# The third attention unit of each layer crosses by DMA transpose, with GpSimd laying its halves apart

## The chip, the cores and the metric

The kernel runs on one core of a Trainium2 chip. The metric is the device time of one execution in microseconds. The four compute engines that matter here are TensorE (PE, with its weight loads PEld), VectorE (DVE), ScalarE (ACT) and GpSimd (POOL); SyncE (SP) issues most of the DMAs. Each engine works through its own queue in order and waits for the others by semaphores.

## The reference

Two decoder layers over 512 tokens of width 1024, all float32. Each layer is a SwiGLU block, a token mixer and a second SwiGLU block, each behind an RMS norm. The mixer projects to queries, keys, values and three convolution parts; 8 query heads of width 64 in 2 groups attend in blocks of 128 tokens to their own block and the one before:

```python
z = h @ w_in[l]
scores = jnp.einsum("bnqkgd,bnskd->bnkgqs", qb, k_band) * scale
scores = jnp.where(mask_b, scores + bias, -jnp.inf)
m = jnp.maximum(jnp.max(scores, axis=-1, keepdims=True), sink_l)
p = jnp.where(mask_b, jnp.exp(scores - m), 0.0)
denom = jnp.sum(p, axis=-1, keepdims=True) + jnp.exp(sink_l - m)
out = jnp.einsum("bnkgqs,bnskd->bnqkgd", p / denom, v_band)
conv_out = short_conv(...)          # B * causal 3-tap convolution of (C * h)
x = x + jnp.concatenate([attn_out, conv_out], axis=-1) @ w_out[l]
```

## The kernel before

Every float32 matrix product is made of three products of a high part (hi, a rounded copy made by ScalarE) and a low part (lo, the rest, made by VectorE): hi·hi, lo·hi and hi·lo. Weights come in by DMA as raw, become wh on ScalarE (L228, CAST) and wl on VectorE (L228, TENSOR_TENSOR), two groups ahead of their use; raw has 8 buffers, which it shares with the attention's probabilities p.

In the mixer the projection runs in steps of one product of 24 matmuls (a group of 128 output columns, L318, L319, L321, into acc). Between the steps the attention's work is laid by tables of step numbers: one *unit* is a block n of 128 queries for one group g of 4 heads. There are 8 units, `todo`, numbered 0 to 3 for group 0 and 4 to 7 for group 1. In the names of tiles a unit is layer_n_g: unit 1 is 0_1_0, unit 2 is 0_2_0, unit 3 is 0_3_0, unit 4 is 0_0_1, unit 5 is 0_1_1. At each step `attend` does, in this order, send, values, turn and scores of the units that the tables name.

- scores: 16 matmuls (L1554, L1555; 8 for block 0) into sc; VectorE adds the bias and takes the maximum (L1558, an ISA row in the order), negates it (nm, L1569), adds the sink (es, L1571); ScalarE takes the exponentials with their sums (L1575); VectorE adds and inverts the sums and scales p (L1583).
- turn: the probabilities are transposed, so that keys lie on the partitions. Units 0, 2, 4, 6 and 7 are turned by TensorE, four transposes of 128x128 for each of their two key blocks (one for block 0; L1616, pt). Units 1, 3 and 5 are sent: ScalarE lays the two 16-bit halves of each word apart (L1590, 128x2048, into crossing), SP issues one DMA transpose back into p (L1592), and at the turn step ScalarE joins the halves of each key block (L1601, 128x1024). Either way ScalarE then makes the high part ph (L1621) and VectorE the low part pl (L1622) for each key block.
- values: two matmuls for each key block, with ph and with pl (L1633, L1634, o); ScalarE copies half of o (ol, L1636), VectorE adds it into m (L1639).

Unit 4's turn is inside the product of step 11 (INSIDE), between two of its k steps. The convolution of the same steps is on VectorE (product with acc, tap L1712), ScalarE (L1709, L1711) and GpSimd (L1715, an add, and L1716, a multiply). A scheduler then orders each engine's queue within what the dependences allow. `issue_after` keeps the joins behind the last weights' cast, and `go_on` keeps the next step's weight splitting behind the last instruction that `attend` gives back.

Of the kernel before, what the change touches and what calls it, by code (L numbers as in the profile page):

```python
# [54 lines left out]
STREAM_BACK_AT = {9: 0, 11: 1, 16: 2, 18: 3}  # L55
SCORES_AT = (5, 6, 7, 8, 9, 10, 12, 13)

SEND_AT = {7: 1, 9: 3, 11: 5}
TURN_AT = (6, 9, 8, 11, 10, 13, 14, 15)
VALUES_AT = (7, 10, 9, 12, 11, 14, 15, 16)  # L60
INSIDE = (11, 4, 5)
WARM = 3
XT_TAGS = ("sc", "aux", "aux", "mm", "sc", "sc", "aux", "aux")
# [12 lines left out]
def trunk_kernel(  # L76
# [23 lines left out]
    nc = tc.nc  # L100
# [11 lines left out]
    def g2(name, dt=F32, shape=(P, S)):  # L112
        return work.tile(list(shape), dt, tag="g2", bufs=14, name=name)

    def g8(name, dt=F32R, shape=(P, 2, 2, S)):
        return work.tile(list(shape), dt, tag="g8", bufs=4, name=name)
# [18 lines left out]
    def words(ap):  # L135

        return ap.bitcast(U16).rearrange("p (n two) -> p two n", two=2)
# [1356 lines left out]
    def mix(l, norm, after):  # L1494
        q = [None] * NH

        mixed = [g8(f"m_{l}_{j}", F32, (P, KC // 2, S)) for j in range(2)]
# [37 lines left out]
        class Unit:  # L1535
# [49 lines left out]
            def send(self):  # L1585


                self.room = crossing[:, todo.index(self) // 2 % 2, :]
                halves = self.room.bitcast(U16).rearrange("p (two n) -> p two n", two=2)
                nc.scalar.copy(halves, words(self.p.rearrange("p h k -> p (h k)")))  # L1590
                self.turned = self.p.rearrange("p h k -> p (h k)").bitcast(U16)
                nc.sync.dma_start_transpose(  # L1592
                    self.turned.rearrange("p (c q) -> p c q", q=P),
                    halves.rearrange("p two n -> p (two n)"),
                )
# [11 lines left out]
            def turn(self):  # L1607

                self.pt = []
                for kb in range(self.lo // P, 2):  # L1610
                    if todo.index(self) in SEND_AT.values():
                        tp = self.join(kb)
# [30 lines left out]
        todo = [Unit(n, g) for g in range(NKV) for n in range(NT)]  # L1643
        crossing = g8(f"crossing_{l}", F32, (P, 2, 4 * 2 * P))

        def attend(step):

            done = None
            if step in SEND_AT:
                todo[SEND_AT[step]].send()  # L1650
            for at, stage in ((VALUES_AT, "values"), (TURN_AT, "turn"), (SCORES_AT, "scores")):
                if stage == "turn" and step + 1 == INSIDE[0]:
                    done = todo[VALUES_AT.index(step)].added
                    continue
                if step in at:
                    done = getattr(todo[at.index(step)], stage)() or done
            return done

        for j in range(NH // 2):
            acc = group(norm.h) if j else qacc  # L1660
            if j == 3:
                vv = take_values()
            qf = scaled(acc, f"qf_{l}_{j}", by=1.0 / 8.0)
            both = form(f"q_{l}_{j}", shape=(P, 2, S))
            qe, qo = both[:, 0, :], both[:, 1, :]
            nc.scalar.copy(qe[:HD, :], qf[:HD, :])
            nc.scalar.copy(qo[HD:, :], qf[HD:, :])
            nc.vector.tensor_sub(qe[HD:, :], qf[:HD, :], f32(qe[:HD, :]))
            nc.vector.tensor_sub(qo[:HD, :], qf[HD:, :], f32(qo[HD:, :]))
            q[2 * j], q[2 * j + 1] = qe, qo  # L1670
            attend(2 + j)
# [4 lines left out]
        step = 6  # L1676
# [9 lines left out]
        def go_on():  # L1686

            nonlocal step
            last = attend(step)
            if step == TURN_AT[-1]:  # L1690
                state["turned"] = last.ins
            step += 1
            with tc.issue_after(last.ins) if last else nullcontext():
                need_split(state["group"] - 1 + SPLIT_AHEAD + (step >= TURN_AT[-1]))

        for pair in range(2):
            cs = []
            for j in range(2):
                c = g2(f"cc_{l}_{pair}_{j}")
# [4 lines left out]
            for j in range(2):  # L1704
                c = 2 * pair + j
# [79 lines left out]
```

## Time and profile before

| | |
|---|---|
| median of 3 runs | 1626.99 us (1626.08 to 1627.02) |
| the profiled execution | 1626.19 us, its span 1624.4 us |
| TensorE's granted clock | 0.999 |
| PE busy | 1615.4 us, 99% |
| DVE busy | 1376.7 us, 85% |
| ACT busy | 1178.1 us, 73% |
| POOL busy | 216.5 us, 13% |
| transposes of p on TensorE (L1616) | 64, median 272 ns each, started back to back |
| sends (L1590), joins (L1601) | 6 of 1897 ns, 12 of 1359 ns |

Times in the timeline are microseconds from the span's start. A line of the timeline has the start, the duration, the engine, the line of the kernel, the operation, its output and input and how often it repeats; in brackets stands idle time of its engine just before it and what ended that. Instructions of one engine overlap a little, so the spacing of their starts is what one of them costs its engine. The first layer's mixer steps discussed here lie at 368 to 440 us, the second's at 1171 to 1243 us.

### The profile page before, as it was taken

What the parts mean: (1) busy time and instruction counts of PE and PEld (TensorE: products, weight loads), DVE (VectorE), ACT (ScalarE), POOL (GpSimd) and SP (SyncE); (2) the same over time, 40 slices, a digit from 0 to 9 for tenths busy, and PEclk for the clock granted to TensorE, in tenths of its full rate; (3) what the DMA queues carried; (4) which work ended last, traced back from release to release, by engine and by line L of the source; (5) the groups of instructions that cost most, each with busy time, mean ns of one, the idle gap of its engine ahead of it and who ended that gap; (6) DMA issues with size and microseconds to landing.
All of it is one profiled execution on the core that took longest, in us unless ns stands there. A gap on an engine that the chain in (4) does not pass through costs nothing.

```text
span 1624.4 us, 21158 instructions
## 1 busy us (share of the span) xinstructions
PE 1615.4 (99%) x7571; PEld 1349.4 (83%) x7571; DVE 1376.7 (85%) x1788; ACT 1178.1 (73%) x1511; POOL 216.5 (13%) x191
## 2 busy tenths in 40 slices
PE   9999999999999999999999999999999999999998
PEld 7888888888898888888888888888888988888887
DVE  7978798988899977798998777989688998678997
ACT  6677777857766677778866777788586767878665
POOL 1211111001211111111011111110012111111121
PEclk9999999999999999999999999999999999999999
DMA  9999989822597698999767999998136978999892
GB/s 270 212 232 209 220 207 226 233 59 78 143 227 175 177 225 214 218 214 225 218 144 182 224 215 226 215 221 217 42 91 156 233 149 219 225 223 222 241 230 72
DMA packets 306031, 313.92 MB, mean 193 GB/s; under 512 B 125501, under 2 KB 188549, under 8 KB 305925
## 3 DMA queue, kind: packets, MB, share of 16 engines
q1 hardware_dynamic: 265412, 230.90, 50.1%
q0 software_dynamic: 40048, 81.27, 29.3%
q8 instruction: 59, 0.97, 0.2%
q14 instruction: 48, 0.39, 0.1%
q10 hardware_dynamic: 464, 0.40, 0.1%
HBM read 264.29 MB, written 2.10 MB: 164 GB/s over the span
## 4 chain that ended last, share of the span: by engine, by line
PE 98%; DVE 1%; DMA 0%; SPq 0%; issue 0%; ACT 0%; DVEq 0%
PE x L842 27%; PE y L842 13%; PE x_s L842 9%; PE acc L318 7%; PE acc L319 7%; PE acc L321 7%; PE w L842 7%; PE y_s L842 5%; PE x_m L827 3%; PE w_s L842 3%; PE y_m L827 1%; PE y_e L842 1%; PE acc L699 1%; PE x_e L842 1%; PE w_m L827 1%; PE sc L1555 0%
## 5 line engine op out<-in xcount | busy, mean ns | idle before, releaser
L228 DVE TENSOR_TENSOR wl<-raw,wh 128x1024 fp32r<-128x1024 f32 (+1 forms) x494 | 598.6, 1219 | 162.8 <-ACT wh L228 161.9
L228 ACT CAST wh<-raw 128x1024 fp32r<-128x1024 f32 (+1 forms) x494 | 514.1, 1044 | 304.6 <-PE x L842 92.8
L318 PE MATMUL acc<-xh,wh 128*128 128x512 f32 x392 | 153.3, 393 | 0.5 <-ACT wh L228 0.5
L319 PE MATMUL acc<-xl,wh 128*128 128x512 f32 x392 | 153.1, 391 | 0.0
L321 PE MATMUL acc<-xh,wl 128*128 128x512 f32 x384 | 149.7, 390 | 0.0
L223 POOL DMA_DIRECT2D raw<-in_ffn_wu_dram x40 | 50.6, 1272 | 381.6 <-DMA raw<-in_ffn_wu_dram 268.6
L318 PEld LDWEIGHTS acc<-xh,wh 128*128 128x128 f32 x392 | 73.8, 188 | 15.0 <-ACT wh L228 0.6
L319 PEld LDWEIGHTS acc<-xl,wh 128*128 128x128 f32 x392 | 73.7, 188 | 14.5
L321 PEld LDWEIGHTS acc<-xh,wl 128*128 128x128 f32 x384 | 72.1, 188 | 15.3
L223 POOL DMA_DIRECT2D raw<-in_ffn_wd_dram x34 | 41.0, 1218 | 272.0 <-DMA raw<-in_ffn_wd_dram 122.3
L223 POOL DMA_DIRECT2D raw<-in_ffn_wg_dram x40 | 49.1, 1237 | 201.9 <-DMA raw<-in_ffn_wu_dram 84.7
L269 DVE TENSOR_TENSOR raw<-raw,raw 128x1024 f32<-128x1024 f32 x58 | 70.5, 1220 | 1.7 <-DMA raw<-in_ffn_wu_dram 1.2
L1106 ACT COPY raw_a<-turned 128x1024 uint16<-128x1024 uint16 x48 | 63.5, 1357 | 0.0
L842 PE MATMUL x<-wl,ft1h 128*128 128x512 f32 x160 | 62.4, 390 | 0.0
L842 PE MATMUL w<-wh,fb21h 128*128 128x512 f32 x160 | 62.3, 390 | 0.0
L842 PE MATMUL y<-wh,ft3h 128*128 128x512 f32 x160 | 62.3, 390 | 0.0
L842 PE MATMUL x<-wh,ft1l 128*128 128x512 f32 x160 | 62.3, 389 | 0.0
L842 PE MATMUL x<-wl,ft2h 128*128 128x512 f32 x160 | 62.3, 389 | 0.0
L842 PE MATMUL x<-wh,ft2l 128*128 128x512 f32 x160 | 62.3, 389 | 0.0
L842 PE MATMUL x<-wh,ft1h 128*128 128x512 f32 x160 | 62.3, 389 | 0.0
L842 PE MATMUL w<-wh,fb21l 128*128 128x512 f32 x160 | 62.2, 389 | 0.0
L842 PE MATMUL y<-wh,ft3l 128*128 128x512 f32 x160 | 62.2, 389 | 0.0
(517 smaller groups left out, 4545.2 us busy)
## 6 DMA issues: line engine op xcount, KB each, us to landing
raw<-in_ffn_wu_dram SPq DMA_DIRECT2D x127, 512.0 KB, 5.6
raw<-in_ffn_wd_dram SPq DMA_DIRECT2D x105, 512.0 KB, 5.6
raw<-in_ffn_wg_dram SPq DMA_DIRECT2D x86, 512.0 KB, 5.3
raw<-in_ffn_wu_dram POOLq DMA_DIRECT2D x40, 512.0 KB, 9.1
raw<-in_ffn_wg_dram POOLq DMA_DIRECT2D x40, 512.0 KB, 6.5
raw<-in_w_in_dram SPq DMA_DIRECT2D x36, 512.0 KB, 4.0
raw<-in_ffn_wd_dram POOLq DMA_DIRECT2D x34, 512.0 KB, 8.2
raw<-in_w_out_dram SPq DMA_DIRECT2D x20, 512.0 KB, 4.6
```

Source lines behind the costliest of these rows:

```text
L223: nc.gpsimd.dma_start(out=r, in_=rows_of(*more), accum_op=ALU.add)
L228: return nc.scalar.copy(hi, raw), eng.tensor_sub(lo, raw, f32(hi))
L269: nc.vector.tensor_add(a11, a11, s1)
L318: nc.tensor.matmul(acc, hi[:, k, :], rhs[k][0], start=k == first, stop=False)
L319: nc.tensor.matmul(acc, hi[:, k, :], rhs[k][1], start=False, stop=False)
L321: nc.tensor.matmul(acc, lo[:, k, :], rhs[k][0], start=False, stop=k == last)
L699: nc.tensor.matmul(opening[n], (lo if part == "w" else hi)[:, k, :], xl if part == "x" else xh, start=n not in begun, stop=k == KC - 1 and ...
L827: nc.tensor.matmul(accs[c // 2][:, c % 2, :], w[:, k, cols], x_[:, 2 * h + k, :], start=start and c % 2 == 0 and h + k + i == 0, stop=h + ...
L842: nc.tensor.matmul(accs[u], x_[:, 2 * h + k, tok], w[:, k, :], start=start and h + k + i == 0, stop=h + k == 2 and i == 2, skip_group_chec ...
L1106: nc.scalar.copy(words(raws[self.b][:, c, :]), self.to[:, :, c, :])
```

## The change

Unit 2 joins the units that are sent. Its halves are laid apart by GpSimd instead of ScalarE (IDLE_LAYS), in a room of its own: the half of `mixed[1]` that the convolution's second pair writes only at steps 16 and 17. It is sent at step 8, turned at step 10 instead of 8, and its values' products are at step 11 instead of 9. `attend` now takes all units that a table names for a step, since two units share a step twice; at step 10 unit 4's turn is still left out there and done inside step 11's product.

```diff
-SEND_AT = {7: 1, 9: 3, 11: 5}
-TURN_AT = (6, 9, 8, 11, 10, 13, 14, 15)
-VALUES_AT = (7, 10, 9, 12, 11, 14, 15, 16)
+SEND_AT = {7: 1, 8: 2, 9: 3, 11: 5}
+TURN_AT = (6, 9, 10, 11, 10, 13, 14, 15)
+VALUES_AT = (7, 10, 11, 12, 11, 14, 15, 16)
+IDLE_LAYS = (2,)
...
-                self.room = crossing[:, todo.index(self) // 2 % 2, :]
+                n = todo.index(self)
+                self.room = crossing[:, n // 2 % 2, :]
+                if n % 2 == 0:
+                    self.room = mixed[1][:, 2:4, :].rearrange("p c s -> p (c s)")
                 halves = self.room.bitcast(U16).rearrange("p (two n) -> p two n", two=2)
-                nc.scalar.copy(halves, words(self.p.rearrange("p h k -> p (h k)")))
+                whole = words(self.p.rearrange("p h k -> p (h k)"))
+                (nc.gpsimd.tensor_copy if n in IDLE_LAYS else nc.scalar.copy)(halves, whole)
...
-                if stage == "turn" and step + 1 == INSIDE[0]:
-                    done = todo[VALUES_AT.index(step)].added
-                    continue
-                if step in at:
-                    done = getattr(todo[at.index(step)], stage)() or done
+                for n in (n for n, when in enumerate(at) if when == step):
+                    if stage == "turn" and n == INSIDE[1]:
+                        done = todo[VALUES_AT.index(step)].added
+                    else:
+                        done = getattr(todo[n], stage)() or done
```

The lines of the code behind these places are 1 to 5 higher in the changed kernel. What this does to the queues of the first layer (the second's are alike):

TensorE before, at the end of step 11's inner product acc_119, where unit 4's products of o stand:

```order
L318 MATMUL acc_119_3648<-xh_1_6_2840,wh_119_3571 128x512
L319 MATMUL acc_119_3648<-xl_1_6_2841,wh_119_3571 128x512
L321 MATMUL acc_119_3648<-xh_1_6_2840,wl_119_3572 128x512
L1633 MATMUL o_0_0_1_3685<-ph_0_0_1_1_3669,vv_0_3202 128x512
L1634 MATMUL o_0_0_1_3685<-pl_0_0_1_1_3670,vv_0_3202 128x512
L318 MATMUL acc_120_3709<-xh_1_0_2886,wh_120_3644 128x512
```

And TensorE now, at the same place:

```order
L319 MATMUL acc_119_3633<-xh_1_6_2840,wh_119_3546 128x512
L320 MATMUL acc_119_3633<-xl_1_6_2841,wh_119_3546 128x512
L322 MATMUL acc_119_3633<-xh_1_6_2840,wl_119_3547 128x512
L1638 MATMUL o_0_2_0_3670<-ph_0_2_0_0_3586,vv_0_3202 128x512
L1639 MATMUL o_0_2_0_3670<-pl_0_2_0_0_3587,vv_0_3202 128x512
L1638 MATMUL o_0_2_0_3670<-ph_0_2_0_1_3591,vv_0_3202 128x512
L1639 MATMUL o_0_2_0_3670<-pl_0_2_0_1_3592,vv_0_3202 128x512
L1638 MATMUL o_0_0_1_3679<-ph_0_0_1_1_3654,vv_0_3202 128x512
L1639 MATMUL o_0_0_1_3679<-pl_0_0_1_1_3655,vv_0_3202 128x512
L319 MATMUL acc_120_3703<-xh_1_0_2886,wh_120_3629 128x512
```

Unit 2's four products came here from the end of the product acc_117, two steps earlier; its eight transposes, which stood inside acc_117, are gone.

ScalarE before, from the exponentials of unit 3 to the second high half of unit 1:

```order
L1575 ACTIVATE p_0_3_0_3446,sums_0_3_0_3465<-p_0_3_0_3446,nm_0_3_0_3461 128x256 x4
L1578 ACTIVATE es_0_3_0_3463<-es_0_3_0_3463 128x4
L1709 ACTIVATE cc_0_0_1_3320<-ch_0_0_1_3483,par_88 128x512
L1711 ACTIVATE tap_0_1_3511<-ch_0_0_1_3483,par_88 128x511
L1636 COPY ol_0_2_0_3523<-o_0_2_0_3518 64x512
L1621 CAST ph_0_1_0_0_3528<-crossing_0_3080 128x512
L1590 COPY crossing_0_3080<-p_0_3_0_3446 128x2048
L1621 CAST ph_0_1_0_1_3533<-crossing_0_3080 128x512
```

And ScalarE now, over the same stretch:

```order
L1576 ACTIVATE p_0_3_0_3430,sums_0_3_0_3449<-p_0_3_0_3430,nm_0_3_0_3445 128x256 x4
L1579 ACTIVATE es_0_3_0_3447<-es_0_3_0_3447 128x4
L229 CAST wh_120_3629<-raw_92_3314 128x1024
L1714 ACTIVATE cc_0_0_1_3320<-ch_0_0_1_3467,par_88 128x512
L1716 ACTIVATE tap_0_1_3495<-ch_0_0_1_3467,par_88 128x511
L1595 COPY crossing_0_3080<-p_0_3_0_3430 128x2048
L1626 CAST ph_0_1_0_0_3503<-crossing_0_3080 128x512
L1576 ACTIVATE p_0_0_1_3513,sums_0_0_1_3532<-p_0_0_1_3513,nm_0_0_1_3528 128x128
L1626 CAST ph_0_1_0_1_3508<-crossing_0_3080 128x512
```

The cast of a weight and one exponential have come into the stretch and the copy of o has left it; the send of unit 3 now stands ahead of both high halves of unit 1.

GpSimd now, from the square of the norm's factor (L1680) on; before, the same rows without the copy:

```order
L1680 TENSOR_TENSOR inv2_0_3244<-inv_1_3011 128x512
L1595 COPY m_0_1_2959<-p_0_2_0_3357 128x2048
L1720 TENSOR_TENSOR cc_0_0_0_3246<-cc_0_0_0_3246,tap_0_0_3422 128x511
L1721 TENSOR_TENSOR cc_0_0_0_3246<-cc_0_0_0_3246,inv_1_3011 128x512
L1720 TENSOR_TENSOR cc_0_0_1_3320<-cc_0_0_1_3320,tap_0_1_3495 128x511
L1721 TENSOR_TENSOR cc_0_0_1_3320<-cc_0_0_1_3320,inv_1_3011 128x512
```

The copy of unit 2's p stands ahead of the four convolution operations of the first pair. On SP's queue the DMA transpose of unit 2 stands between that of unit 1 and that of unit 3, and one load of w_in that stood ahead of unit 3's transpose now stands behind it.

## The prediction

> **What bounds the kernel now.** I read the page first: the busy times and the chain that ended last.
>
> ```profile
> PE 1615.4 (99%) x7571; PEld 1349.4 (83%) x7571; DVE 1376.7 (85%) x1788; ACT 1178.1 (73%) x1511; POOL 216.5 (13%) x191
> ...
> PE 98%; DVE 1%; DMA 0%; SPq 0%; issue 0%; ACT 0%; DVEq 0%
> ```
>
> TensorE is busy in 1615.4 of 1624.4 us and is 98% of the chain. So the time falls only by work that TensorE no longer does, and rises by every wait put in front of it. The 73% of ScalarE is a mean over stages, so I asked for the windows around the third unit's old and new place in the first layer.
>
> ```profile
> 390.00:400.00 10.00, 10.00 (x53) 8.40 (x52) 8.61 (x25) 8.62 (x20) 2.76 (x3) 1.00 0.37 107
> 400.00:410.00 10.00, 10.00 (x51) 8.14 (x50) 9.91 (x34) 9.67 (x20) 2.75 (x2) 1.00 0.25 58
> ```
>
> The columns are PE, PEld, DVE, ACT and POOL. ScalarE is busy in 18.29 of these 20 us and VectorE in 18.52: in this stage neither has much left. Next, who keeps TensorE waiting, and TensorE's timeline at the places that change (o are the values' products).
>
> ```profile
> PEld o L1634 <- DVE pl L1622: 1.4, 5, 0.4
> ```
>
> ```profile
> 389.35 0.39 PE L321 MATMUL acc<-xh,wl 128*128 128x512 f32 x1
> 389.57 0.40 PE L318 MATMUL acc<-xh,wh 128*128 128x512 f32 x1
> 389.81 1.12 PE L1616 MATMUL pt<-ident,p 128*128 128x128 f32 x8
> 390.69 0.48 PE L319 MATMUL acc<-xl,wh 128*128 128x512 f32 x1
> 391.01 0.39 PE L321 MATMUL acc<-xh,wl 128*128 128x512 f32 x1
> ...
> 402.62 0.39 PE L1633 MATMUL o<-ph,vv 128*128 128x512 f32 x1
> 402.85 0.39 PE L1634 MATMUL o<-pl,vv 128*128 128x512 f32 x1
> ...
> 403.43 0.50 PE L1634 MATMUL o<-pl,vv 128*128 128x512 f32 x1
> ...
> 410.90 0.39 PE L1634 MATMUL o<-pl,vv 128*128 128x512 f32 x1
> ```
>
> Matmuls start 0.23 us apart. The four products at 402.62 are unit 1's, and the fourth, due at 403.31, starts at 403.43: it is already held by VectorE's low half pl. So even now a DMA-turned unit is just in time.
>
> **Term 1, TensorE sheds the transposes.** From the product at 389.57 to the second one behind it (391.01) is 1.44 us with eight transposes between; two steps without them are 0.46. Gone: 0.98 us a layer. Unit 2's four products move behind unit 1's, 4 x 0.23 = 0.91 us, neither gained nor lost. Together TensorE would reach unit 1's fourth product 1.89 us earlier, at 401.42.
>
> **Term 2, when unit 1's halves are ready.** ScalarE's timeline before:
>
> ```profile
> 387.94 1.05 ACT L228 CAST wh<-raw 128x1024 fp32r<-128x1024 f32 x1
> 388.89 1.37 ACT L1601 COPY crossing<-p 128x1024 uint16<-128x1024 uint16 x1
> 390.12 0.71 ACT L1709 ACTIVATE cc<-ch,par 128x512 f32<-128x512 f32 x1
> ...
> 395.10 0.51 ACT L1575 ACTIVATE p<-p,nm 128x256 f32<-128x256 f32 x1 [1.33 <-DVE nm L1569]
> ...
> 398.52 0.59 ACT L1636 COPY ol<-o 64x512 f32<-64x512 f32 x1
> 399.01 0.62 ACT L1621 CAST ph<-crossing 128x512 fp32r<-128x512 f32 x1
> 399.53 1.90 ACT L1590 COPY crossing<-p 128x2048 uint16<-128x2048 uint16 x1
> 401.33 0.62 ACT L1621 CAST ph<-crossing 128x512 fp32r<-128x512 f32 x1
> ```
>
> By their starts a weights' cast takes 0.95, a join half 1.23, ol 0.49, ph 0.52, a send 1.80. From unit 3's exponentials (395.10) to unit 1's second ph (401.33) are 6.23 us. In the new order this stretch loses ol of unit 2 (0.49) and gains a weights' cast (0.95) and the first exponential of unit 4 (half as wide as the 0.51 at 395.10; I take 0.40): 7.09. When does it begin? At unit 3's nm on VectorE, and that depends on GpSimd:
>
> ```profile
> 399.82 1.29 POOL L1715 TENSOR_TENSOR cc<-cc,tap 128x511 f32<-128x511 f32 x1 [4.79 <-issue]
> 393.74 1.29 POOL L1716 TENSOR_TENSOR cc<-cc,inv 128x512 f32<-128x512 f32 x1
> ```
>
> ```profile
> 385.50 0.17 DVE L1569 TENSOR_SCALAR nm<-mx 128x4 f32<-128x4 f32 x1
> 389.19 1.13 DVE L1583 TENSOR_SCALAR p<-p,sums 128x256 f32<-128x256 f32 x4
> 391.48 0.75 DVE L1712 SCALAR_TENSOR_TENSOR tap<-ch,par,tap 128x510 f32<-128x510 f32 x1 [0.34 <-ACT tap L1711]
> 392.75 0.48 DVE L1558 CUSTOM_DVE_ANT_0 p<-sc,bias,sink 128x256 f32<-128x256 f32 x1
> 394.40 0.66 DVE L1569 TENSOR_SCALAR nm<-mx 128x4 f32<-128x4 f32 x1
> 400.48 1.18 DVE L1622 TENSOR_TENSOR pl<-crossing,ph 128x512 fp32r<-128x512 f32 x1
> 402.40 0.97 DVE L1622 TENSOR_TENSOR pl<-crossing,ph 128x512 fp32r<-128x512 f32 x1
> ```
>
> The nm of 385.50 took 0.17 us, that of 394.40 took 0.66 and ended at 395.06, just after GpSimd's multiply (393.74 + 1.29 = 395.03). A pl of 1.18 us ran into the add of 399.82; the scores' reduction at 392.75, with one input in PSUM, was not slowed. So GpSimd's operation holds such VectorE operations until it ends. The Trainium skill, "SBUF — State Buffer", section "Who interferes with whom", calls it an exclusive lock that the first holds for its whole instruction; the rows agree for operations of 1.29 us, and no run here shows a longer one. By that rule a longer copy blocks in full length, which speaks against this change; if GpSimd let VectorE in between, the sum would be that of the second rival.
>
> The new copy is ready when unit 2's p is: 390.3 before (389.19 + 1.13), some 0.9 later now, since a weights' low half stands ahead of unit 2's nm and reductions ahead of the scaling: about 391.2. The convolution's tap stands directly behind the scaling on VectorE and starts first: copy from 391.9. Its price isn't in the trace. Nearest rows:
>
> ```profile
> L173 POOL CAST ones_r<-ones 128x128 fp32r<-128x128 f32 x1 | 0.3, 288 | 0.0
> L441 POOL MEMSET eps<- 128x1 f32 x1 | 0.1, 96 | 0.0
> ```
>
> One input, 128 elements: 288 ns, 96 of them fixed by the smallest row, so 1.5 ns an element and 3.1 us for 2048. Lower bound: ScalarE's 1.90 for the same form. Upper: four times the two-input 1.29, 5.2. I take 3.1, the row of GpSimd's own one-input operation. By the Trainium skill, "GPSIMD Engine Reference", section 4.1, one-input operations run at roughly line rate; with its clock and 1.03 cycles an element that would be an estimated 1.8 us, and the sum near +2.5.
>
> So the copy ends at 395.0, nm behind it (and queued behind nm on VectorE the convolution's second product and unit 3's scaling, for which ScalarE's send waits); the exponentials start at 395.25: no earlier than before, although TensorE comes 1.89 earlier. The second ph starts at 395.25 + 7.09 = 402.34 and ends at 402.96; pl (0.69 alone) would end at 403.75, but the second convolution multiply falls on unit 1's first pl as the add did before, up to 0.65 more. I take 404.2 for the fourth product. TensorE waits 404.2 - 401.42 = 2.8 us.
>
> **Term 3, the next wait.** From the fourth product to unit 4's second is 7.47 us (403.43 to 410.90), now 8.38 with unit 2's four products between: 412.6. ScalarE's row from the second ph: three exponentials and es 1.3, four join halves 4.9 (two of them new), ol 0.5, two ph 1.0, a cast 0.95, then unit 4's ph: starts 402.86 + 8.65 = 411.5, ends 412.1. VectorE behind it: a reduction pair after unit 2's pl, a weights' low half, then unit 4's pl: ends about 413.4. TensorE waits 0.9 more. After that unit 3's halves come just in time.
>
> **What else moves.** Unit 2's p holds its buffer two steps longer; unit 5's reduction now waits for the second join half of unit 2, which the row above already has. On SP's queue one load of w_in falls behind two transposes:
>
> ```profile
> 390.96 5.62 SPq L210 DMA_DIRECT2D raw<-in_w_in_dram  x2
> ...
> 416.54 1.06 ACT L228 CAST wh<-raw 128x1024 fp32r<-128x1024 f32 x1 [0.70 <-PE acc L319]
> ```
>
> ```profile
> raw<-in_w_in_dram SPq DMA_DIRECT2D x36, 512.0 KB, 4.0
> ...
> p<-crossing SPq DMA_TRANSPOSE x6, 3.7
> ```
>
> It was issued by 396.6 and is read at 416.54. Now it waits for a low half at some 405, lands 4.0 later: still 7 us early. If that cover were gone, each us late is a us of TensorE. Unit 2's transposed half lands 3.7 after its issue, at about 399, and ScalarE takes it at 404.1. GpSimd's convolution operations come 2.7 us behind the copy's end, at 397.7, and VectorE reads the first at 404.58:
>
> ```profile
> 404.58 0.68 DVE L1720 TENSOR_TENSOR m<-acc,cc 128x512 f32<-128x512 f32 x1
> ```
>
> All three cost nothing.
>
> **The sum.** Per layer -0.98 - 0.12 (the old wait) + 2.8 + 0.85 = +2.55. The second layer stands alike:
>
> ```profile
> 392.37 1.29 POOL L1715 TENSOR_TENSOR cc<-cc,tap 128x511 f32<-128x511 f32 x1 [46.29 <-DVE tap L1712]
> 1195.09 1.30 POOL L1715 TENSOR_TENSOR cc<-cc,tap 128x511 f32<-128x511 f32 x1 [46.25 <-DVE tap L1712]
> ```
>
> so +5.1 in all: the profiled execution's 1626.19 (span 1624.4) becomes 1631.3, and the median of the runs, 0.80 above it, 1626.99 becomes 1632.1. All later terms shift with the copy's end: at 1.9 us for the copy it is +2.7 (1629.7), at 5.2 +9.3 (1636.3).
>
> **Rivals.** *No wait takes the place* (the other side): ScalarE has its halves ready in time, because its idle gaps (1.33 before 395.10) absorb the work. TensorE then sheds 1.96 us: 1625.0; with the 1.4 us of waits gone as well, 1623.6. It decides if unit 1's last pl is done by 401.4, 2 us before the old one. For it: gaps exist, and nothing but TensorE is on the chain. Against: 1.7 us of ScalarE's 20 are free and the new order needs 2.5 more for two join halves.
>
> *GpSimd doesn't hold VectorE, or copies quickly.* Unit 3's nm comes at once, and the exponentials start when ScalarE is free, about 393.7, 1.55 earlier than I take: +1.0 a layer, 1629.0. For it: the copy has one input, and no row shows one this long. Against: nm at 394.40.
>
> *The copy runs at the two-input price.* Then the joins and unit 3 wait 2.1 us longer a layer: 1636.3. For it: strided 16-bit words; against: the cast row.
>
> **How the numbers follow.** Forecast 0.55, its own range 1629.7 to 1635; no wait 0.15; free or quick GpSimd 0.17; slow copy 0.13. The range to 0.2% of 1626.99, 3.25 us, is about what a measurement of this kernel can tell from no change. Slower than 1630.24: 0.48 of the forecast and the slow copy, 0.61. Within: 0.07 of the forecast, 0.17, and 0.10 of the no-wait case, 0.34. Faster: the 0.05 in which the old waits go too. From 1624.5 to 1636.0 leaves out that 0.05 and about 0.08 of the slow copy.
>
> **What would show it.** In the profile after: L1638 and L1639 products of o waited for by pl or ph, some 2.8 and 0.9 us a layer, about 7 us in all where 1.4 stood; a GpSimd copy of 128x2048 of 3 us; behind it an nm of over 2 us; TensorE's transposes 48 instead of 64. Wrong if the o products wait for less than 1 us a layer, if the copy takes under 2 us, or if a weights' cast waits for its DMA.

## The result and the profile after

The changed kernel takes 1628.93 us (median of 22 runs, 1627.99 to 1631.23) where the kernel before takes 1626.29 us (22 runs, 1625.55 to 1628.49): +2.64 us, ratio 1.0016, 95% interval 1.0010 to 1.0022. That is slower, by about half of the +5.1 that was forecast, and below the forecast's own range of 1629.7 to 1635. The page of the profile after, its span 1626.2 us:

```profile
PE 1614.5 (99%) x7555; PEld 1346.9 (83%) x7555; DVE 1383.9 (85%) x1788; ACT 1182.3 (73%) x1515; POOL 220.1 (14%) x193
...
PE 96%; DVE 2%; ACT 1%; DMA 0%; issue 0%; SPq 0%; DVEq 0%; ACTq 0%
```

TensorE has 16 instructions less and is busy 0.9 us less, and the share of VectorE and ScalarE in the chain that ended last has gone from 1% to 3%: TensorE waits. The waits name the place, the values' products:

```profile
PEld o L1639 <- DVE pl L1627: 5.7, 8, 1.7
```

It was 1.4 us before, and the prediction had about 7. The windows around the change in the first layer (PE, PEld, DVE, ACT, POOL, then the granted clock) show which engine has filled up. The kernel before, over the 30 us from 388 to 418:

```profile
388.00:418.00 30.00, 30.00 (x152) 24.96 (x151) 26.67 (x78) 27.48 (x53) 5.51 (x4) 1.00 0.38 102
```

The kernel after:

```profile
388.00:418.00 30.00, 28.63 (x135) 22.91 (x134) 27.35 (x76) 29.57 (x57) 7.38 (x5) 1.00 0.39 105
390.00:400.00 10.00, 10.00 (x50) 8.38 (x49) 9.43 (x26) 9.65 (x17) 6.11 (x5) 1.00 0.24 55
400.00:410.00 10.00, 8.69 (x44) 6.82 (x43) 9.92 (x24) 9.95 (x19) 1.27 (x1) 1.00 0.42 107
```

TensorE goes from 30.00 busy to 28.63; ScalarE from 27.48 to 29.57, which leaves it no gap.

To follow one layer I set the clock to zero at unit 1's first score. Before, the two ends of the stretch are:

```profile
374.11 0.28 PE L1554 MATMUL sc<-kh,q 128*128 128x256 f32 x1
...
431.23 1.04 PE L1616 MATMUL pt<-ident,p 128*128 128x128 f32 x8
```

After, with the products of unit 1 (400.18 to 402.48), unit 4's second (411.08) and two of unit 3's (417.23 and 418.07) between them:

```profile
373.54 0.28 PE L1555 MATMUL sc<-kh,q 128*128 128x256 f32 x1
...
400.18 0.39 PE L1638 MATMUL o<-ph,vv 128*128 128x512 f32 x1
401.87 0.50 PE L1639 MATMUL o<-pl,vv 128*128 128x512 f32 x1 [1.31 <-DVE pl L1627]
402.21 0.40 PE L1638 MATMUL o<-ph,vv 128*128 128x512 f32 x1
402.48 0.50 PE L1639 MATMUL o<-pl,vv 128*128 128x512 f32 x1
...
411.08 0.50 PE L1639 MATMUL o<-pl,vv 128*128 128x512 f32 x1
...
417.23 0.50 PE L1639 MATMUL o<-pl,vv 128*128 128x512 f32 x1
...
418.07 0.50 PE L1639 MATMUL o<-pl,vv 128*128 128x512 f32 x1
...
431.90 1.03 PE L1621 MATMUL pt<-ident,p 128*128 128x128 f32 x8
```

The stretch was 57.12 us and is 58.36, +1.24; in the second layer 57.09 and 58.39, +1.30. Together +2.54, nearly all of the measured +2.64. Step by step in the first layer: unit 1's first product comes 1.87 earlier (26.64 for 28.51), its last only 0.38 earlier (28.94 for 29.32), so 1.49 is lost in waiting there. Unit 2's four products follow (4 x 0.23), and unit 4's second product is 0.75 late (37.54 for 36.79), 0.22 of it new. At unit 6's first transposes the delay is 1.24; the last 0.5 is lost between, at unit 3's products.

What they wait for is on VectorE, ScalarE and GpSimd. VectorE after:

```profile
390.57 0.74 DVE L1717 SCALAR_TENSOR_TENSOR tap<-ch,par,tap 128x510 f32<-128x510 f32 x1
...
391.75 1.33 DVE L1570 TENSOR_SCALAR nm<-mx 128x4 f32<-128x4 f32 x1
...
398.77 1.16 DVE L1570 TENSOR_SCALAR nm<-mx 128x4 f32<-128x4 f32 x1
...
400.04 2.38 DVE L1627 TENSOR_TENSOR pl<-crossing,ph 128x512 fp32r<-128x512 f32 x2
...
410.33 0.69 DVE L1627 TENSOR_TENSOR pl<-pt,ph 128x512 fp32r<-128x512 f32 x1
```

GpSimd after:

```profile
390.80 2.26 POOL L1595 COPY m<-p 128x2048 uint16<-128x2048 uint16 x1 [45.29 <-DVE p L1584]
...
399.98 1.29 POOL L1721 TENSOR_TENSOR cc<-cc,inv 128x512 f32<-128x512 f32 x1
```

ScalarE after:

```profile
391.96 1.03 ACT L229 CAST wh<-raw 128x1024 fp32r<-128x1024 f32 x1
393.12 0.51 ACT L1576 ACTIVATE p<-p,nm 128x256 f32<-128x256 f32 x1
...
400.02 0.40 ACT L1576 ACTIVATE p<-p,nm 128x128 f32<-128x128 f32 x1 [0.24 <-DVE nm L1570]
400.42 0.60 ACT L1626 CAST ph<-crossing 128x512 fp32r<-128x512 f32 x1
...
409.64 0.59 ACT L1626 CAST ph<-pt 128x512 fp32r<-128x512 f32 x1
```

GpSimd's copy holds unit 3's nm until 393.06 as forecast, but ScalarE is busy with a weights' cast until 392.99 anyhow, so the hold costs it about 0.1 us. The convolution's second multiply holds unit 1's first pl until 401.27: two pl take 2.38 us where 0.69 is the time of one that is not held. From 393.12 to 418 ScalarE has one gap of more than 0.1 us, that of 0.24.

### The profile page after: what moved, and what is told of

Same layout as the page of the kernel before. It is cut to its first block, busy times and chain, and to the rows that moved or that the text cites. A ratio compares the mean times of both kernels' runs of the same rounds, so it can differ in the third digit from the quotient of the medians.

```text
span 1626.2 us, 21139 instructions
## 1 busy us (share of the span) xinstructions
PE 1614.5 (99%) x7555; PEld 1346.9 (83%) x7555; DVE 1383.9 (85%) x1788; ACT 1182.3 (73%) x1515; POOL 220.1 (14%) x193
## 4 chain that ended last, share of the span: by engine, by line
PE 96%; DVE 2%; ACT 1%; DMA 0%; issue 0%; SPq 0%; DVEq 0%; ACTq 0%
PE x L843 27%; PE y L843 13%; PE x_s L843 9%; PE acc L319 7%; PE acc L320 7%; PE w L843 7%; PE acc L322 7%; PE y_s L843 5%; PE w_s L843 3%; PE x_m L828 3%; PE y_m L828 1%; PE y_e L843 1%; PE x_e L843 1%; PE acc L700 1%; PE w_m L828 1%; PE acc L338 0%
## 5 line engine op out<-in xcount | busy, mean ns | idle before, releaser
L843 PE MATMUL x<-wh,ft2h 128*128 128x512 f32 x160 | 62.3, 389 | 0.0
```

The source lines that it names most:

```text
L843: nc.tensor.matmul(accs[u], x_[:, 2 * h + k, tok], w[:, k, :], start=start and h + k + i == 0, stop=h + k == 2 and i == 2, skip_group_chec ...
```

## The experiments

Twelve kernels, each timed beside the kernel before, with 5 or 11 runs. Differences are of medians, against the kernel before that was timed beside it; the intervals reach 1.3 to 2.3 us either way, and those of the kernels without the transposes, without the second channel's GpSimd work and with both edits take in no change at all. So the traces' checkpoints carry the argument. Each is of one profiled execution, and they repeat between the layers to 0.1 us unless said. The first layer, us after unit 1's first score, each worked out from the starts in that kernel's timeline as above:

| kernel | unit 1's first product | unit 1's last | unit 4's last | unit 6's transposes | both layers against before | median against before |
|---|---|---|---|---|---|---|
| before | 28.51 | 29.32 | 36.79 | 57.12 | | |
| after | 26.64 | 28.94 | 37.54 | 58.36 | +2.54 | +2.64 |
| no transposes, nothing moved | 27.97 | 29.88 | 37.35 | 57.69 | +1.15 | +0.74 |
| moved, turned by TensorE | 26.64 | 28.49 | 37.74 | 58.10 | +2.03 | +1.52 |
| second channel's GpSimd work out | 26.63 | 27.93 | 37.13 | 58.05 | +1.85 | +1.37 |
| joins out | 26.64 | 28.94 | 37.34 | 57.99 | +2.09 | +1.78 |
| both out | 26.61 | 27.90 | 36.27 | 56.95 | -0.29 | -0.44 |
| ScalarE lays | 26.64 | 28.47 | 36.99 | 59.38 | +4.63 | +5.70 |
| VectorE lays | 26.64 | 28.40 | 37.11 | 58.67 | +3.06 | +2.97 |

**The transposes alone.** The kernel before without unit 2's eight transposes:

```diff
-                        for h in range(4):
+                        for h in range(4) if todo.index(self) != 2 else ():
...
+                        if todo.index(self) == 2:
+                            tp = self.p[:, :, kb * P : (kb + 1) * P]
```

> The kernel before with unit 2's eight TensorE transposes left out (its halves are taken from p as it stands, so unit 2's products are computed from unturned values). It prices the first term of the prediction by itself. By that term: -0.98 us a layer, -1.96 us in all, and the waits for pl at unit 1's fourth product grow by at most 0.3 us a layer: -1.4 to -2.0. Rival, TensorE only comes earlier to a wait that takes the whole gain: within 0.5 us of the kernel before, with 1 us a layer more of waits at the products of o.

Measured +0.74 us (1.0005, 0.9996 to 1.0014), by the trace +0.57 a layer. The first term's saving isn't seen: TensorE sheds 0.98 us a layer and gains none of it. The rival comes nearer, but not even it had a loss of this size. The scheduler also set a weights' cast between unit 1's two high halves, as ScalarE's timeline of this kernel shows:

```profile
401.55 0.62 ACT L1623 CAST ph<-crossing 128x512 fp32r<-128x512 f32 x1
402.07 1.05 ACT L228 CAST wh<-raw 128x1024 fp32r<-128x1024 f32 x1
403.02 0.62 ACT L1623 CAST ph<-crossing 128x512 fp32r<-128x512 f32 x1
```

and ScalarE had waited before that:

```profile
398.04 0.72 ACT L1711 ACTIVATE cc<-ch,par 128x512 f32<-128x512 f32 x1 [1.32 <-DVE ch L1709]
```

So the last product comes 0.56 later than before (29.88 for 29.32), and that is the loss: here the time is set by when unit 1's halves are ready, not by TensorE's work. It isn't a clean price of the transposes. Unit 2's pl now reads p and ph instead of pt and ph, beside it GpSimd's add and multiply took 1.62 and 1.69 us for 1.29, and behind them VectorE's es took 1.25 and the ch that ScalarE waited for came late. What the gain would be without that was not seen.

**The move alone.** The changed kernel's tables, but unit 2 turned by TensorE, at its new steps:

```diff
-SEND_AT = {7: 1, 8: 2, 9: 3, 11: 5}
+SEND_AT = {7: 1, 9: 3, 11: 5}
```

> The move alone: unit 2 is turned by TensorE as before, but at step 10, with its products at step 11; no DMA transpose, no GpSimd copy, no two join halves. Theory 1 (the joins on ScalarE and the copy on GpSimd make the waits): the move costs nothing, within 0.5 us of the kernel before, waits for pl at the products of o 0.5 us a layer at most. Rival, the later place makes the wait (the weights' casts and unit 3's send stand ahead of unit 1's halves because unit 2 is no longer there): +2 to +4.6 us, since the 0.98 a layer of the transposes is not saved here, and the wait at unit 1's products stays at 1 us or more a layer.

Measured +1.52 us (1.0009, 1.0000 to 1.0018). My theory that the move is free fell. The rival's wait is there (28.49 for 26.64 + 0.69, 1.16 a layer), and its time of +2 or more by the trace (+2.03), though not by the median. Its TensorE timeline:

```profile
402.61 0.50 PE L1639 MATMUL o<-pl,vv 128*128 128x512 f32 x1 [0.87 <-DVE pl L1627]
```

The eight transposes and four products of unit 2, 1.89 us, stood ahead of unit 1's products and covered the time until its halves were ready. Behind them they cover nothing: TensorE arrives 1.87 early, gets 0.83 of it (28.49 for 29.32), and still has the 1.89 to do. So of the +2.54, about 2.0 is the move; the DMA turn on top of it saves 1.96 of transposes and loses 2.5 elsewhere. The rival's reason doesn't hold as it stands: the halves come earlier than before, not later.

**Without the holds of the second convolution channel.**

```diff
-                nc.gpsimd.tensor_add(y[:, 1:], y[:, 1:], tap[:, 1:])
-                nc.gpsimd.tensor_mul(y, y, norm.inv)
+                if c != 1:
+                    nc.gpsimd.tensor_add(y[:, 1:], y[:, 1:], tap[:, 1:])
+                    nc.gpsimd.tensor_mul(y, y, norm.inv)
```

> The changed kernel without GpSimd's two operations of the convolution's second output channel (an add and a multiply of 1.29 us, left out, so that channel's values are not finished). They held nm of unit 4 until 399.9 and the first pl of unit 1 until 401.27 in the changed kernel. Theory 1 (held VectorE operations are what unit 1's products wait for in the end): the first pl ends about 1.2 us earlier, the wait of 1.31 us falls to 0.3 or less: -1.5 to -2.4 against the changed kernel, so 0 to +1 against the kernel before. Theory 3 (ScalarE's row alone sets pl, whose last half is made from the second ph): the wait stays over 0.9 us and the kernel at +2 or more.

Measured +1.37 us (1.0008, 0.9999 to 1.0017), above the 0 to +1 of my theory, whose wait of 0.3 or less at unit 1 holds. Unit 1's last product comes 1.01 earlier than in the changed kernel; its wait of 1.31 is gone, and 0.18 is left at the last product. But at unit 6 only 0.31 of the 1.01 remains. ScalarE's windows say why:

```profile
388.00:418.00 30.00, 29.44 (x138) 23.35 (x137) 25.41 (x75) 29.82 (x60) 4.80 (x3) 1.00 0.41 109
```

ScalarE, at 29.82 of 30 us, makes the high halves of unit 4 and unit 3 only 0.3 earlier, so the time comes back as waits there. The edit takes out two holds, that of unit 4's nm and that of unit 1's pl, and doesn't tell them apart.

**Without the joins.** Unit 2's halves from unit 1's room:

```diff
-                    if todo.index(self) in SEND_AT.values():
+                    if todo.index(self) == 2:
+                        tp = todo[1].room[:, kb * 4 * P : (kb + 1) * 4 * P].rearrange("p (h q) -> p h q", h=4)
+                    elif todo.index(self) in SEND_AT.values():
```

> The changed kernel with unit 2's two join halves on ScalarE left out (its high and low halves are made from unit 1's joined halves instead, so unit 2's products are not its own); GpSimd's copy and the DMA transpose stay. Numbers against the kernel before, to which the changed kernel stands at +2.6. Theory 1 (two costs: TensorE comes early to unit 1's products, about 1.3 to 1.6 us a layer, and ScalarE has no room for the joins, 0.7 a layer behind that): the second goes and the first stays: +0.6 to +1.6. Rival A (the joins on ScalarE are the whole cost): -1 to -2. Rival B (GpSimd's hold of VectorE is the whole cost, the joins only fill time): unchanged, +2 to +3.

Measured +1.78 us (1.0011, 1.0002 to 1.0020), a little above what I gave. The products of unit 1 wait exactly as in the changed kernel:

```profile
403.49 0.50 PE L1641 MATMUL o<-pl,vv 128*128 128x512 f32 x1 [1.31 <-DVE pl L1629]
```

and the wait at unit 4 is gone (37.34, which is 28.94 and 8.40 without a pause). Rival A falls: the joins are not the whole cost. Rival B the total can't exclude (+2.09 by the trace lies in its +2 to +3); against it speaks only that the joins do cost a little, 0.37 in the first layer and 0.1 in the second, where unit 3's pl came later.

**Both out.** The two edits above together.

> As the kernel without the joins (unit 2's halves made from unit 1's), and the second convolution channel's add and multiply on GpSimd left out too. Theory 1 (the held low half of unit 1 is the larger part of its wait, the joins the later one): both go, and most of the 0.98 us a layer of the transposes is seen: -0.8 to -2.0. Rival (what remains of unit 1's wait is its place in ScalarE's row, which neither edit moves): 0 to +1.

Measured -0.44 us (0.9997, 0.9988 to 1.0006), by the trace -0.29: 2.8 to 3.1 us better than the changed kernel, where the two edits alone gave 0.7 and 0.5 by the trace. They stand one behind the other: each is hidden as long as the other is there. The bound that I gave (-0.8 to -2.0) was too good: 0.60 of waits and restarts is left at unit 1's products (27.90 for 26.61 + 0.69), of it

```profile
402.09 0.50 PE L1641 MATMUL o<-pl,vv 128*128 128x512 f32 x1 [0.18 <-DVE pl L1629]
```

behind the second high half, so its place in ScalarE's row remains, and 0.35 more is lost behind unit 4.

**ScalarE lays the halves apart.**

```diff
-IDLE_LAYS = (2,)
+IDLE_LAYS = ()
```

> The changed kernel with unit 2's halves laid apart by ScalarE (about 1.9 us a layer there) instead of GpSimd (2.27 us). The numbers are against the kernel before, to which the changed kernel stood at +2.6 us. Theory 1, the wait at unit 1's products comes from GpSimd holding VectorE and from ScalarE's longer row together: nm of unit 3 is held no more (0.2 instead of 1.33 us), but ScalarE's row is 1.9 longer ahead of unit 1's last ph, so the wait there grows by 0.5 to 1.9 us a layer: +3.5 to +6.5 us. Theory 2, the copy's hold on VectorE is the whole cause: the wait at unit 1's products falls below 0.5 us a layer and the kernel stands at 0 to -2. Theory 3, ScalarE's row is the whole cause: the full 1.9 a layer is added, +6.4 or more, and nm's wait plays no part.

Measured +5.70 us (1.0035, 1.0022 to 1.0049): 1.9 us more on ScalarE a layer costs 1.05 a layer by the trace, though no GpSimd copy holds VectorE any more. That the copy's hold is the whole cause falls. Theory 1 has the number and not the place: unit 1's last product comes 0.47 earlier than in the changed kernel (28.47 for 28.94). The loss moved to unit 3's products, and some 0.4 a layer to unit 7's last product, behind the stretch of the table (the waits for pl come to 7.8 us in all):

```profile
PEld o L1639 <- DVE pl L1627: 7.8, 12, 1.3
```

**VectorE lays them apart.**

```diff
-                (nc.gpsimd.tensor_copy if n in IDLE_LAYS else nc.scalar.copy)(halves, whole)
+                (nc.vector.tensor_copy if n in IDLE_LAYS else nc.scalar.copy)(halves, whole)
```

> The changed kernel with unit 2's halves laid apart by VectorE instead of GpSimd. No GpSimd copy holds nm of unit 3 (1.33 us) any more; VectorE has one copy more, of 0.6 to 2 us. In the changed kernel ScalarE's weights' cast ended 0.13 us before unit 3's exponentials began, so Theory 1 (ScalarE's row is what counts there, and the hold lay beside it) gives no more than 0.3 us a layer: +2 to +3.2 against the kernel before. Rival (the hold of nm is what the change costs): 0 to +1.

Measured +2.97 us (1.0020, 1.0012 to 1.0029), as by my theory, but it is a weaker test than I meant. VectorE's timeline and GpSimd's:

```profile
391.73 1.22 DVE L1595 COPY m<-p 128x2048 uint16<-128x2048 uint16 x1
...
393.38 0.73 DVE L1570 TENSOR_SCALAR nm<-mx 128x4 f32<-128x4 f32 x1
```

```profile
391.95 2.14 POOL L1720 TENSOR_TENSOR cc<-cc,tap 128x511 f32<-128x511 f32 x1 [45.95 <-DVE tap L1717]
```

Now VectorE's copy holds GpSimd's add (2.14 us for 1.29), and the add, ended at 394.09, holds nm. So what a free nm would be worth was not seen.

**The copy twice.**

```diff
                 (nc.gpsimd.tensor_copy if n in IDLE_LAYS else nc.scalar.copy)(halves, whole)
+                if n in IDLE_LAYS:
+                    nc.gpsimd.tensor_copy(halves, whole)
```

> The changed kernel with GpSimd's copy of unit 2 issued twice, 2.27 us a layer more. It prices the slope that the prediction gave to the copy's length (every us of copy a us of wait). By that slope: unit 3's nm held to about 395.3, its exponentials and all of ScalarE's row behind them 2.2 us later, +2.0 to +2.3 a layer, so +6.6 to +7.2 against the kernel before. Rival (the copy ends beside ScalarE's other work, and only a part counts): +3 to +5.

Measured +6.64 us (1.0040, 1.0028 to 1.0053): the number of the prediction's slope, by luck, since its mechanism is another. GpSimd, VectorE and TensorE:

```profile
393.69 1.29 POOL L1722 TENSOR_TENSOR cc<-cc,tap 128x511 f32<-128x511 f32 x1
394.92 1.89 POOL L1597 COPY m<-p 128x2048 uint16<-128x2048 uint16 x1
```

```profile
397.26 1.74 DVE L1584 TENSOR_SCALAR p<-p,sums 128x256 f32<-128x256 f32 x4
```

```profile
403.60 0.52 PE L1641 MATMUL o<-pl,vv 128*128 128x512 f32 x1 [1.58 <-DVE pl L1629]
```

The second copy was put behind the convolution's add, after nm. It held unit 3's sums and scaling instead (1.74 for 1.14), ScalarE's send waited 0.9 us for them, unit 1's last product came 1.17 later than in the changed kernel, and then TensorE ran at half clock for some 3 us. The windows of this kernel, the granted clock in the third column from the end:

```profile
402.00:404.00 2.00, 0.41 (x3) 0.30 (x2) 2.00 (x2) 2.00 (x11) 1.00 (x1) 0.99 1.13 258
404.00:406.00 2.00, 2.00 (x9) 1.71 (x8) 2.00 (x5) 2.00 (x4) 0.00 (x0) 0.50 0.03 4
406.00:408.00 2.00, 2.00 (x9) 1.71 (x8) 1.92 (x8) 2.00 (x3) 0.00 (x0) 0.66 0.71 206
```

So the slope of the copy's length was not tested.

**GpSimd joins unit 2.**

```diff
-                    nc.scalar.copy(
+                    (nc.gpsimd.tensor_copy if todo.index(self) in IDLE_LAYS else nc.scalar.copy)(
```

> The changed kernel with unit 2's two join halves on GpSimd instead of ScalarE (2.45 us a layer less on ScalarE, which was busy in 29.57 of 30 us from 388 to 418 in the changed kernel and in 27.48 before). Numbers against the kernel before, to which the changed kernel stands at +2.6. Theory 1, two causes one after the other: unit 1's products are waited for because their halves stand in ScalarE's queue behind unit 3's exponentials and send (the joins come after them and play no part), and units 4 and 3 are waited for because ScalarE's row has no room left for the joins. Then unit 1's wait of about 1.3 us a layer stays and the later 0.7 a layer goes: +0.6 to +1.6. Rival, GpSimd's hold of VectorE is what counts: two more GpSimd copies of about 1.2 us each hold VectorE's low halves and its weights' low half near 402 to 405 us, so the waits grow: +3 to +5.

Measured +7.82 us (1.0046, 1.0033 to 1.0059), over both theories. GpSimd and VectorE:

```profile
397.13 2.80 POOL L1606 COPY m<-p 128x1024 uint16<-128x1024 uint16 x2 [1.10 <-DMA p<-m]
```

```profile
396.48 2.24 DVE L1584 TENSOR_SCALAR p<-p,sums 128x256 f32<-128x256 f32 x4
```

The joins came as soon as the transpose had landed, earlier than on ScalarE, and held unit 3's scaling (2.24 for 1.14); its send waited 0.9 us, and unit 1's products 2.1:

```profile
403.81 0.50 PE L1639 MATMUL o<-pl,vv 128*128 128x512 f32 x1 [2.08 <-DVE pl L1627]
```

The rival's mechanism holds, at another operation than the one it named. By the same stretch of the two layers this profiled execution was only 4.9 us behind the kernel before; it is the shortest of five, which spread to 1635.33. TensorE's granted clock was 1.000 over this one and 0.995 to 0.997 over the four longer ones; where they lost it, no trace shows.

**Unit 1's halves earlier.** Its joins are done by 392.1, and its high halves stand behind unit 3's exponentials and send; one step earlier they stand ahead:

```diff
-TURN_AT = (6, 9, 10, 11, 10, 13, 14, 15)
+TURN_AT = (6, 8, 10, 11, 10, 13, 14, 15)
```

> The changed kernel with one number changed: unit 1's turn stage at step 8 instead of 9, so that its two high halves stand ahead of unit 3's exponentials on ScalarE. The work is the same. Theory 1 (unit 1's halves wait for their place in the queue): the wait at unit 1's products, 1.3 to 1.6 us a layer, goes; since ScalarE has no room left, part of it comes back at units 4 and 3 (as 0.7 of 1.1 did without the second channel's GpSimd operations): 0 to +1.9 against the kernel before. Rival, ScalarE's sum of work alone decides and the order does not: within 0.5 us of the changed kernel, +2.1 to +3.1, the waits only moved to units 4 and 3.

Measured +7.59 us (1.0047, 1.0034 to 1.0061); both expectations fell. VectorE and TensorE:

```profile
394.71 1.78 DVE L1627 TENSOR_TENSOR pl<-crossing,ph 128x512 fp32r<-128x512 f32 x1
396.42 1.21 DVE L229 TENSOR_TENSOR wl<-raw,wh 128x1024 fp32r<-128x1024 f32 x1
```

```profile
397.69 0.51 PE L322 MATMUL acc<-xh,wl 128*128 128x512 f32 x1 [1.89 <-DVE wl L229]
```

The waits at unit 1's products are gone, but its second pl now meets the convolution's multiply on GpSimd, and behind it in VectorE's queue stands the weights' low half that TensorE needs next: a wait of 1.89 at the projection. After it the clock falls. The windows:

```profile
398.00:400.00 2.00, 2.00 (x7) 1.58 (x6) 2.00 (x12) 1.73 (x3) 0.00 (x0) 0.64 0.00 0
400.00:402.00 2.00, 2.00 (x6) 1.52 (x6) 2.00 (x6) 2.00 (x2) 0.95 (x1) 0.51 0.00 0
```

(1 - 0.64) x 2 + (1 - 0.51) x 2 is 1.7 us lost in each such place, nearly as much as the wait.

**The same in two other kernels.** Unit 1's turn at step 8 in the kernel whose unit 2 is only moved, and together with the joins on GpSimd; to the diffs of those two kernels comes in both

```diff
-TURN_AT = (6, 9, 10, 11, 10, 13, 14, 15)
+TURN_AT = (6, 8, 10, 11, 10, 13, 14, 15)
```

> The move alone (unit 2 turned by TensorE, at step 10, its products at step 11), which stood at +1.5 by the median and +1.0 a layer by the profile, with unit 1's turn stage at step 8. Theory 1 (the move's price is that TensorE comes 1.9 us early to unit 1's products, whose halves stand where they stood in ScalarE's queue): without that wait the move costs nothing: -0.5 to +0.5. Rival (the later place of unit 2 itself costs, on its own halves or on those of unit 4): it stays at +1 to +2.

> Both at once: unit 1's turn stage at step 8 and unit 2's joins on GpSimd. Theory 1: no wait of more than 0.3 us is left at any product, and the 0.98 a layer of the transposes is gained: -1 to -2 against the kernel before. Rival (GpSimd's hold): the joins on GpSimd hold VectorE's low halves of units 2 and 4: +1 to +3.

Measured +8.60 us (1.0052, 1.0039 to 1.0064) and +11.62 us (1.0071, 1.0058 to 1.0083): the theory and the rival fell in both. Each has a wait for a weights' low half at the projection, the first with its line here and the second below:

```profile
396.90 0.50 PE L322 MATMUL acc<-xh,wl 128*128 128x512 f32 x1 [1.23 <-DVE wl L229]
```

```profile
399.91 0.80 PE L322 MATMUL acc<-xh,wl 128*128 128x512 f32 x1 [2.97 <-DVE wl L229]
```

In the first that wait is not the larger loss. Unit 1's last product is 0.29 later than with the move alone (28.78 for 28.49), and unit 4's last 1.63 (39.37 for 37.74), so most is lost between the two.

No version that computes the whole was faster than the kernel before.

## Why the prediction was right and where it was off

The direction was right and the size twice the measured one. The prediction gave 0.61 to a time above 1630.24 and 0.34 to one within 0.2% of the old median, where 1628.93 lies. Of its signs, the waits for pl came to 5.7 us for about 7, the copy to 2.26 for 3, the nm behind it to 1.33 for over 2, and the transposes to 48.

**What bounds the kernel**: right. TensorE sheds work and the time does not fall, since it waits for unit 1's halves; the transposes-out kernel shows it without any DMA turn, though with side effects of its edit.

**Term 1**: right. Unit 1's first product comes 1.87 us earlier (forecast 1.89), with 48 transposes.

**Term 2**, a wait of 2.8 us at unit 1's products: TensorE comes early to halves that don't, as written; the size is off, and the step that failed is the copy's price. TensorE could have made the fourth product at 26.64 + 0.69 = 27.33 and made it at 28.94: 1.61. The copy was put at 3.1 us by the cast row of 128 elements and took 2.26, of which some 0.4 waited for the convolution's tap on VectorE; where the tap came after it, as in GpSimd's timeline of the kernel with unit 1's turn at step 8,

```profile
390.39 1.88 POOL L1595 COPY m<-p 128x2048 uint16<-128x2048 uint16 x1 [44.40 <-DVE p L1584]
```

the same copy took 1.88. The tap ended when it was forecast to (391.31 - 373.54 = 17.77, where the copy was to start at 391.9 - 374.11 = 17.79), so the copy's price alone made it end 1.37 earlier than forecast (393.06 - 373.54 = 19.52 for 395.0 - 374.11 = 20.89), and unit 3's exponentials began 1.56 earlier. From there to the second high half are 7.30 us for 7.09, and the multiply falls on the first pl as forecast. The fourth product was put 0.77 later than before (404.2 for 403.43) and came 0.38 earlier. At 1.9 us for the copy the prediction's own sum gave +2.7. By the estimate from the Trainium skill, "GPSIMD Engine Reference", section 4.1, it was 1.8 us and about +2.5; the 1.88 of the unheld copy agrees with it, and the cast row was the wrong neighbour.

That the hold sets the start of ScalarE's row was right by 0.1 us only: at 2.26 us the copy ends just when ScalarE's weights' cast does. In the move alone, where GpSimd copies nothing, 1.16 of the 1.61 are waited as well, so the copy and what comes with it cost 0.45 a layer there and TensorE's early arrival the rest. The Trainium skill's rule in "SBUF — State Buffer", section "Who interferes with whom", is borne out for the longer operation: a copy of 2.26 us held an nm of 128x4 to its end.

**Term 3**, 0.85 at unit 4: 0.22. "After that unit 3's halves come just in time" failed the other way: 0.5 is lost there. The two together are 0.7, so the cost was summed nearly right and put at the wrong product. ScalarE's row from unit 1's second high half to unit 4's, put at 8.65, took 8.7 (400.93 to 409.64); the step that was off is VectorE's pl of unit 4, put 1.3 behind the end of that high half and ended 0.8 behind it. The kernel without the joins shows that the joins are the cause at unit 4.

**Costed at nothing**: the moved load, the landing of unit 2's transpose and the later results of GpSimd's convolution work made no wait of TensorE in this stretch of the changed kernel. But "4 x 0.23, neither gained nor lost" hides the step that the sum had right without naming it: the move alone is +2.0 us.

**Rivals**: no wait takes the place: fell. A slow copy: fell. Of the rival "GpSimd doesn't hold VectorE, or copies quickly" the second half came true: it had the exponentials start at 393.7, which is 19.59 on this clock, and they started at 19.58. The holds stayed. That its 1629.0 is nearly the measured 1628.93 is partly luck: as a difference it is +2.0 for +2.64, and the kernel before came out 0.70 below the median that it was reckoned from.

## What to carry to other kernels

Before work is taken from a bound engine, ask what it is waiting beside: work that stands ahead of a consumer whose inputs come at a fixed time is free cover, and taking or moving it away gains nothing until the inputs come earlier. When two waits stand one behind the other, remove both in an experiment before judging either: alone they gave 0.7 and 0.5 us here, together 2.8. Moving one operation forward on one engine's queue moves what follows it on the next engine's: look there for who stands behind it.

## What the hardware showed that I had not expected

Short waits of TensorE can cost twice. After a wait of 1.89 us, and after one of 1.58 behind one of 0.5, the granted clock of the first layer was 0.50 to 0.66 for two windows of 2 us, with matmuls of 0.63 us for 0.39; after 2.97 us, in the kernel with both unit 1's earlier turn and the joins on GpSimd, it was 0.50 to 0.54 for three. After 1.31 us in the changed kernel, and after 2.08 behind 0.53 in the profiled execution of the kernel whose joins are on GpSimd, it stayed at 1.00; over that kernel's other four runs it was 0.995 to 0.997, so the same kernel can go either way. The Trainium skill, "TensorE: Matmul & The Clock Gate", section "Why this matters for your kernels", warns of gaps of more than about 3 us; here less sufficed, and length alone did not decide.

The hold between GpSimd and VectorE goes both ways: VectorE's copy of 1.22 us made GpSimd's 1.29 us add take 2.14. The same copy of 128x2048 16-bit words was 1.22 us on VectorE, 1.88 to 2.28 on GpSimd and 1.89 on ScalarE.
